# Gate and up projections of an FFN as seven-product 2x2 block multiplications, with hidden tiles and x1 in DRAM

## The chip, the cores and the metric

The kernel runs on one core of one Trainium2 chip. The metric is the device time of one execution in microseconds (us). Engines are named as the profile names them: PE is TensorE (matmuls; PEld its weight loads), DVE is VectorE, ACT is ScalarE, POOL is GpSimd, SP is SyncE, which only issues DMAs here. ACT issues DMAs too.

## The reference, cut to what matters

One layer of an encoder for 1024 prompt tokens and 64 sample tokens, which the kernel treats as one axis of 1088 tokens. Three token mixers (stick-breaking attention, RG-LRU, memory attention) are merged and projected; the change touches what follows:

```
x = x + merged @ lw["w_out"]                     # 1088 x 1024
xn2 = rms_norm(x, lw["norm_ffn_g"])
f = (silu(xn2 @ w_ffn_gate) * (xn2 @ w_ffn_up)) @ w_ffn_down   # hidden width 2816 = 22 x 128
x = x + f
```

## The kernel before

Activations lie feature-major: 8 tiles of 128 features x 1088 tokens. Every fp32 operand is split into a high and a low part (`split`, L68 and L69: ACT casts, DVE subtracts), and a product is three matmuls: high x high, high x low, low x high (`mm3`, L97 to L99). A projection tile (`proj`) is 128 output features: 3 column chunks of 364, 364 and 360 tokens, 8 contraction blocks and 3 matmuls, 72 in all.

The stages run one after the other: attention, RG-LRU, memory attention, branch merge, w_out, FFN. The program is written in that order, and a scheduler sets the order of instructions on each engine from data dependences, buffers and priorities; what each engine then does is fixed, in order. Names of tiles: `wo0` to `wo7` are the weights of the eight w_out tiles, `fg`, `fu` and `fd` those of gate, up and down; a last letter r is the raw load, h and l are the two parts. `xr` is a block of the input x, transposed by PE into `xtp` and copied by ACT to `mg`; `xrs` is that of the sample tokens.

In w_out (L926 to L958) each tile's evacuation adds the product to `mg` (x1), scales and splits it into `xg`, and POOL sums the squares in `ssq`. `token_scale` makes from these the 1/rms of each token, `R`: PE sums over features (`stp`), POOL takes the power (`rt`), PE spreads it (`rbp`). `raw` buffers, of which there are three, hold `ssq`, the `xr` blocks and raw weights. In the FFN gate and up tiles alternate; gate's evacuation is times R and Silu, up's is times R, times gate's tile on POOL, and split into `hh` and `hl`. After 6, 6, 6 and 4 hidden tiles the down projection of that group is added to `mg`; with the last group each tile is transposed (`ytp`) and stored.

## Time and profile before

| | us |
|---|---|
| timed runs | 2463.35, 2464.81, 2465.91 (median 2464.81) |
| profiled execution, span | 2465.6 |
| PE busy in the span | 2422.1 |
| DVE, ACT, POOL busy in the span | 1063.9, 850.3, 391.4 |

The span is that of the instructions of one execution, and it lies within the timed runs, so nothing of note lies around it. Busy shares are averages over stages with different limits; PE's matmul records overlap their successors, so that the rate is read from starts and not from durations.

### The profile page before, as it was taken

The page shows a single profiled execution, that of the slowest core. Times are in us where ns is not written, and L with a number is a line of the kernel's source. Part 1 is how long each engine was busy: PE and PEld are TensorE (multiplying, and loading weights), DVE is VectorE, ACT ScalarE, POOL GpSimd, SP SyncE. Part 2 cuts the span into 40 slices and gives each one's busy share as a digit, 9 for nine tenths or more (in the row PEclk, how much of TensorE's full clock was granted, in tenths as well). Part 3 has the DMA queues.
Part 4 walks back from the last instruction along what each step waited for, and adds up shares of the span by engine and source line. Part 5 has one row for each costly group of instructions (what it writes and reads, how often), then busy time and mean ns, then how long its engine had stood idle before and what let it go on. Part 6 is the DMA issues. An engine that isn't in the chain of part 4 may idle for free.

```text
span 2465.6 us, 36133 instructions
## 1 busy us (share of the span) xinstructions
PE 2422.1 (98%) x15030; PEld 2375.9 (96%) x15030; DVE 1063.9 (43%) x1715; ACT 850.3 (34%) x1484; POOL 391.4 (16%) x448
## 2 busy tenths in 40 slices
PE   7999999999999999999999999999999999999999
PEld 7899999989999999999989999999999999999999
DVE  4666666664555543333444323343323332332332
ACT  4555555554345333332354323222211221121112
POOL 3222222211112110100100222341100110010010
PEclk9999999999999999999999999999999999999999
DMA  4111111122322322222335432221111111111103
GB/s 144 55 56 56 56 56 56 56 69 81 106 85 87 105 88 92 85 78 93 109 117 175 148 100 83 80 79 43 42 39 58 43 35 52 44 46 39 53 26 90
DMA packets 281016, 185.16 MB, mean 75 GB/s; under 512 B 13059, under 2 KB 275414, under 8 KB 280854
## 3 DMA queue, kind: packets, MB, share of 16 engines
q10 hardware_dynamic: 209982, 108.36, 15.3%
q1 hardware_dynamic: 70872, 74.50, 9.3%
q8 instruction: 118, 1.93, 0.3%
q14 instruction: 44, 0.36, 0.0%
...
## 4 chain that ended last, share of the span: by engine, by line
PE 77%; DVE 1%; ACT 0%; issue 0%; POOL 0%; DMA 0%; ACTq 0%; DVEq 0%
PE mm L97 23%; PE mm L99 23%; PE mm L98 23%; PE mmk L97 1%; PE mmk L98 1%; PE mmk L99 1%; PE ytp L1033 0%; PE sc L97 0%; PE avm L97 0%; PE sc L98 0%; PE sc L99 0%; PE ptp L785 0%; PE gt L99 0%; PE gt L97 0%; PE avm L99 0%; PE avm L98 0%
## 5 line engine op out<-in xcount | busy, mean ns | idle before, releaser
L1006 POOL TENSOR_TENSOR ut<-ut,sil 128x364 f32<-128x364 f32 (+1 forms) x66 | 64.2, 973 | 670.1 <-DVE ut L1005 661.0
L1022 DVE TENSOR_TENSOR mg<-mg,mm 128x364 f32<-128x364 f32 (+1 forms) x96 | 51.1, 532 | 183.7 <-PE mm L99 183.7
L987 DVE TENSOR_TENSOR sil<-mm,R 128x364 f32<-128x364 f32 (+1 forms) x66 | 35.2, 535 | 163.3 <-PE mm L99 163.3
L68 ACT CAST hh<-ut 128x364 fp32r<-128x364 f32 (+1 forms) x66 | 32.8, 497 | 191.6 <-POOL ut L1006 191.6
L370 DVE TENSOR_TENSOR_SCAN e<-ones,e 128x128 f32<-128x128 f32 (+3 forms) x64 | 97.1, 1526 | 0.8
L852 POOL TENSOR_TENSOR mg<-mg,sig 128x364 f32<-128x364 f32 (+1 forms) x48 | 46.3, 968 | 286.1 <-DVE sig L851 286.1
L206 DVE TENSOR_SCALAR gst<-mm,prm 128x364 f32<-128x364 f32 (+1 forms) x71 | 42.0, 592 | 103.5 <-PE mm L99 103.5
L988 ACT ACTIVATE sil<-sil 128x364 f32<-128x364 f32 (+1 forms) x66 | 33.3, 506 | 128.2 <-DVE sil L987 128.1
L369 DVE SCALAR_TENSOR_TENSOR e<-z,e 128x384 f32<-128x384 f32 (+4 forms) x96 | 50.4, 553 | 61.3 <-ACT e L367 57.6
L1005 DVE TENSOR_TENSOR ut<-mm,R 128x364 f32<-128x364 f32 (+1 forms) x66 | 35.4, 536 | 95.8 <-PE mm L99 95.8
L846 ACT ACTIVATE sig<-sig 128x364 f32<-128x364 f32 (+1 forms) x72 | 35.8, 507 | 113.4 <-DMA sig<-g 102.5
L69 DVE TENSOR_TENSOR hl<-ut,hh 128x364 fp32r<-128x364 f32 (+1 forms) x66 | 35.1, 532 | 75.2 <-ACT hh L68 75.2
L374 ACT ACTIVATE e<-e 128x128 f32<-128x128 f32 (+3 forms) x64 | 43.9, 686 | 60.1 <-DVE e L373 52.3
L69 DVE TENSOR_TENSOR al<-at,ah 128x128 fp32r<-128x128 f32 (+2 forms) x96 | 51.1, 547 | 20.6 <-ACT ah L68 20.6
L97 PE MATMUL z<-kh,qh 128*128 128x384 f32 (+4 forms) x96 | 36.5, 380 | 14.7 <-DVE e L373 14.7
L365 ACT ACTIVATE e<-z 128x384 f32<-128x384 f32 (+4 forms) x96 | 45.7, 484 | 10.6 <-PE z L99 7.6
L373 DVE TENSOR_TENSOR e<-z,e 128x384 f32<-128x384 f32 (+4 forms) x96 | 48.9, 542 | 0.0
L98 PE MATMUL av<-al,vh 128*128 128x256 f32 x160 | 46.7, 292 | 0.2
L97 PE MATMUL av<-ah,vh 128*128 128x256 f32 x160 | 46.4, 290 | 0.4 <-ACT ah L68 0.4
L851 DVE TENSOR_TENSOR sig<-sig,mm 128x364 f32<-128x364 f32 (+1 forms) x48 | 25.2, 531 | 49.8 <-PE mm L99 49.7
L423 PE MATMUL at<-ident,e 128*128 128x128 f32 x288 | 45.1, 275 | 1.4 <-ACT ah L68 0.6
L68 ACT CAST ah<-at 128x128 fp32r<-128x128 f32 (+2 forms) x96 | 43.0, 471 | 10.0 <-PE at L423 10.0
...
## 6 DMA issues: line engine op xcount, KB each, us to landing
...
```

The lines of the kernel that those rows point to most:

```text
L68: (h_eng or S.copy)(h, src)
L69: (l_eng or V).tensor_sub(l, src, f32(h))
L97: TE.matmul(out, lh, rh, start=start, stop=False)
L98: TE.matmul(out, lh, rl, start=False, stop=False)
L99: TE.matmul(out, ll, rh, start=False, stop=stop)
L365: S.activation(ev, z, AF.Abs)
L369: V.scalar_tensor_tensor(ev, z, 0.0, ev, op0=ALU.max, op1=ALU.add)
L370: V.tensor_tensor_scan(e[:, ::-1], ones1[:n].to_broadcast([n, L]), e[:, ::-1], 0.0, op0=ALU.mult, op1=ALU.add)
L373: V.tensor_sub(ev, z, ev)
L852: G.tensor_add(dst, dst, st[:, :n])
L1006: G.tensor_mul(u, u, t)
L1022: V.tensor_add(mg[f][:, s:s + n], mg[f][:, s:s + n], p)
```

## The change

The gate and up weights of two neighbouring tiles (256 output features) and the 8 contraction blocks are taken as a 2x2 block matrix: A11, A12, A21, A22, where the first index is the output tile and the second parts even from odd contraction blocks. The activations are a 2x2 block matrix too: even and odd contraction blocks, and the two token halves of 544. Seven products of sums of these blocks (`PAIRS`) replace eight. The weight sums S1 to S4 and the activation sums T1 to T4 are formed on DVE in fp32 and then split as before. Each product has 2 column halves of 272 tokens, 4 contraction blocks and 3 matmuls; partial results are kept by ACT copies (`swt`) or accumulate in PSUM.

The 28 activation operands (7 kinds x 4) fill the tiles A and most of B, so the hidden tiles go to DRAM (`hid_scr`) and come back for the down projection, now in groups of 8, 8 and 6; x1 goes to `x1_scr` and comes back as `y`. The scaled x1 lies in `mg`, for the last two tiles in two `raw` buffers (`xg6`, `xg7`). The gate and up weights are loaded on SP's queue instead of ACT's, 256 features at a time. `form_early` runs with every second w_out tile, `form_late` behind the last. A parameter of the program that sets a scratch size for DMAs changes too.

```diff
+    PAIRS = (("A11", "B11"), ("S3", "T3"), ("S2", "T2"), ("A22", "T4"), ("S1", "T1"), ("A12", "B21"), ("S4", "B22"))
+    def sw_weights(src, name, slot, stage):
+        n = src.shape[0] // (2 * P)
+        v = src.rearrange("(i two p) f -> two p i f", two=2, p=P)
+        quads = {}
+        for r in range(2):
+            st = stage(f"{name}r{r}")[:, : 2 * n * P].rearrange("p (i f) -> p i f", i=n)
+            ST.dma_start(st, v[r])
+            quads[f"A1{r + 1}"], quads[f"A2{r + 1}"] = st[:, :, :P], st[:, :, P:]
+        for r in range(2):
+            st = stage(f"{name}s{r}")[:, : 2 * n * P].rearrange("p (x i f) -> p x i f", x=2, i=n)
+            for x, o in enumerate((("S3", "S2"), ("S1", "S4"))[r]):
+                quads[o] = st[:, x]
+        W = {}
+        def put(o):
+            w = W[o] = slot(f"{name}{o}")[:, : 2 * n * P].rearrange("p (x i f) -> p x i f", x=2, i=n)
+            split(w[:, 0], w[:, 1], quads[o])
+        put("A11")
+        V.tensor_sub(quads["S3"], quads["A11"], quads["A21"])
+        put("S3")
+        V.tensor_sub(quads["S2"], quads["A22"], quads["S3"])
+        put("S2")
+        V.tensor_add(quads["S1"], quads["A22"], quads["A21"])
+        put("A22")
+        put("S1")
+        V.tensor_sub(quads["S4"], quads["A12"], quads["S2"])
+        put("A12")
+        put("S4")
+        return W
+    def sw_product(W, X, n, banks, temp, out):
+        def run(op, bank, start):
+            a, b = PAIRS[op]
+            for c in range(2):
+                cs = slice(c * HC, (c + 1) * HC)
+                for i in range(n):
+                    w, x = W[a], X[b][i]
+                    for j, (wj, xj) in enumerate(((0, 0), (0, 1), (1, 0))):
+                        TE.matmul(bank[c][:, :HC], w[:, wj, i], x[:, xj, cs], start=start and i == 0 and j == 0,
+                                  stop=i == n - 1 and j == 2, skip_group_check=True)
+                yield c
+        def keep(bank, c, j):
+            with tc.high_priority():
+                S.copy(tmp[c][:, j], bank[c][:, :HC])
+        def done(f, half, bank, c, j):
+            with tc.high_priority():
+                out(f, half, c, bank[c][:, :HC], None if j is None else tmp[c][:, j])
+        bx, bw = banks(), banks()
+        tmp = [temp()[:, : 4 * HC].rearrange("p (j n) -> p j n", j=4) for _ in range(2)]
+        for c in run(0, bx, True):
+            keep(bx, c, 0)
+        for c in run(1, bw, True):
+            keep(bw, c, 1)
+        for c in run(2, bx, False):
+            keep(bx, c, 2)
+        for c in run(3, bw, False):
+            done(1, 0, bw, c, 2)
+        for c in run(4, bx, False):
+            done(1, 1, bx, c, 1)
+        by = banks()
+        for c in run(5, by, True):
+            done(0, 0, by, c, 0)
+        for c in run(6, bx, False):
+            done(0, 1, bx, c, None)
...
+        def operand(o, i, src):
+            t = XS[o][i] = at(xg_place[o, i], f"xg{o}{i}").rearrange("p (x n) -> p x n", x=2)
+            split(t[:, 0], t[:, 1], src)
+        def stage_x(name):
+            return wpl.tile([P, HT], F32, tag="stg", name=name, bufs=3)
+        def form_early(i, x0, x1):
+            operand("B11", i, x0[:, :HT])
+            t3, t2, t4 = (stage_x(f"t{j}{i}") for j in (3, 2, 4))
+            V.tensor_sub(t3, x1[:, HT:], x0[:, HT:])
+            operand("T3", i, t3)
+            V.tensor_add(t2, t3, x0[:, :HT])
+            operand("T2", i, t2)
+            V.tensor_sub(t4, x1[:, :HT], t2)
+            operand("T4", i, t4)
+        def form_late(i, x0, x1):
+            t1 = stage_x(f"t1{i}")
+            V.tensor_sub(t1, x0[:, HT:], x0[:, :HT])
+            operand("T1", i, t1)
+            operand("B21", i, x1[:, :HT])
+            operand("B22", i, x1[:, HT:])
...
+            ST.dma_start(x1_scr[f], mg[f])
+            x = mg[f]
+            if f >= KT - 2:
+                x = wpl.tile([P, T], F32, tag="raw", name=f"xg{f}", bufs=RAWB)
+            S.activation(x, mg[f], AF.Copy, scale=gk)
+            xg.append(x)
+            if f % 2 == 1:
+                form_early(f // 2, xg[f - 1], xg[f])
+        for i in range(KT // 2):
+            form_late(i, xg[2 * i], xg[2 * i + 1])
+        R = mgp.tile([P, T], F32, tag="mg0", name="R")
...
+        W_PLACES = [(wpl, "wh"), (wpl, "wl"), (wpl, "wh"), (wpl, "wl")] + PB[12:14]
+        STAGE_PLACES = [(wpl, "wx"), (wpl, "wx"), (wpl, "wx"), (mgp, "mg1"), (wpl, "wx"), (wpl, "wx"), (wpl, "wx"), PB[14]]
...
+        def temp():
+            return wpl.tile([P, T], F32, tag="raw", name="swt", bufs=RAWB)
+        def banks4():
+            pool, tag = cycle("b", [(psm, "mm"), (ps, "mm"), (ps, "mm"), (ps, "tr")])
+            return [pool.tile([P, 512], F32, tag=tag, name="sw", bufs=4 if pool is ps and tag == "mm" else 2)
+                    for _ in range(2)]
...
+        def up_pair(j, W, sil):
+            u = [at(cycle("u", U_PLACES), f"u{j}{f}", F32) for f in range(2)]
+            def out(f, half, c, p, other):
+                s = slice(half * HT + c * HC, half * HT + (c + 1) * HC)
+                t = u[f][:, s]
+                if other is None:
+                    V.tensor_mul(t, p, R[:, s])
+                else:
+                    V.tensor_add(t, p, other)
+                    G.tensor_mul(t, t, R[:, s])
+                V.tensor_mul(t, t, sil[f][:, s])
+            sw_product(W, XS, KT // 2, banks4, temp, out)
+            for f in range(2):
+                ST.dma_start(hid_scr[2 * j + f], u[f])
+        w = ffn_weights(w_ffn_gate, 0, "fg")
+        token_scale()
+        for j in range(NH // 2):
+            wu = ffn_weights(w_ffn_up, j, "fu")
+            sil = gate_pair(j, w)
+            if j + 1 < NH // 2:
+                w = ffn_weights(w_ffn_gate, j + 1, "fg")
+            up_pair(j, wu, sil)
+        groups = [list(range(0, 8)), list(range(8, 16)), list(range(16, 22))]
...
+        def load_h(j):
+            q = 2 * (j % 16)
+            Hh[j] = at((PA + PB)[q], f"hh{j}")
+            Hl[j] = at((PA + PB)[q + 1], f"hl{j}")
+            raw = wpl.tile([P, T], F32, tag="wx", name=f"hr{j}", bufs=3)
+            ST.dma_start(raw, hid_scr[j])
+            split(Hh[j], Hl[j], raw)
+        for j in groups[0]:
+            load_h(j)
+        mg = []
+        for f in range(KT):
+            mg.append(mgp.tile([P, T], F32, tag=f"mg{f}", name=f"y{f}"))
+            ST.dma_start(mg[f], x1_scr[f])
...
-    nc = bacc.Bacc("TRN2", target_bir_lowering=False, num_devices=1)
+    nc = bacc.Bacc("TRN2", target_bir_lowering=False, num_devices=1, dynamic_dma_scratch_size=2048)
```


Three places where the order of instructions differs. Names are as above; a number behind a name counts buffers.

ACT, around the turn from w_out's seventh tile (wo6) to its eighth (wo7). Before:

```order
L68 CAST wo6h_15735<-wo6r_15733 128x1024
L930 DMA xr7_15832<-in_x_prompt_dram 128x8x128
L948 ACTIVATE xgh5_15000<-mg5_9648,prm_150 128x364
L941 COPY mg6_9649<-xtp_15718 128x512
L948 ACTIVATE xgh5_15000<-mg5_9648,prm_150 128x360
L932 DMA xrs6_15716<-in_x_sample_dram 64x128
L941 COPY mg6_9649<-xtp_15724 128x512
L76 DMA wo7r_15851<-in_w_out_dram 128x8x128
L941 COPY mg6_9649<-xtp_15730 128x64
L948 ACTIVATE xgh6_15001<-mg6_9649,prm_150 128x364
L68 CAST wo7h_15853<-wo7r_15851 128x1024
```


After:

```order
L1064 COPY mg6_9649<-xtp_15774 128x64
L1083 ACTIVATE xg6_15871<-mg6_9649,prm_150 128x1088
L1053 DMA xr7_15873<-in_x_prompt_dram 128x8x128
L1055 DMA xrs7_15875<-in_x_sample_dram 64x128
L72 CAST xgB113_15988<-xg6_15871 128x544
L1064 COPY mg7_9650<-xtp_15877 128x512
L1064 COPY mg7_9650<-xtp_15883 128x512
L1064 COPY mg7_9650<-xtp_15889 128x64
L80 DMA wo7r_15892<-in_w_out_dram 128x8x128
L72 CAST wo7h_15894<-wo7r_15892 128x1024
L72 CAST fg0A11_16057<-fg0r0_16051 128x512
```


The load xr7 stood before, behind the cast of wo6, and wo7r amid the copies for wo6. Now the load xr7 stands behind the scaling that makes xg6 from the finished mg6, and wo7r behind the three copies of xr7's transposes, directly ahead of its cast.

PE, from the sums of squares to the spread of R. Before, with the first matmuls of up tile 0 (fu0) between:

```order
L967 MATMUL stp_16034<-ones1_82,ssq_15011 64x1
L97 MATMUL mm_16080<-xgh0_14995,fu0h_16076 128x364
L98 MATMUL mm_16080<-xgl0_15003,fu0h_16076 128x364
L99 MATMUL mm_16080<-xgh0_14995,fu0l_16077 128x364
L97 MATMUL mm_16080<-xgh1_14996,fu0h_16076 128x364
L98 MATMUL mm_16080<-xgl1_15004,fu0h_16076 128x364
L978 MATMUL rbp_16051<-ident_70,rt_16048 128x128 x4
L978 MATMUL rbp_16057<-ident_70,rt_16048 128x128 x4
```


After, a piece of the first gate pair, with the products of S2, A22 and S1 (the letters and digits behind fg0 name the weight block, xgT and the like the activation operand):

```order
L226 MATMUL sw_16148<-xgT22_15751,fg0S2_16065 128x272 x3
L226 MATMUL sw_16148<-xgT23_15999,fg0S2_16065 128x272 x3
L226 MATMUL sw_16150<-xgT40_15263,fg0A22_16069 128x272 x2
L226 MATMUL sw_16147<-xgT10_16008,fg0S1_16072 128x272 x2
L226 MATMUL sw_16148<-xgT10_16008,fg0S1_16072 128x272 x2
L226 MATMUL sw_16149<-xgT40_15263,fg0A22_16069 128x272
L226 MATMUL sw_16149<-xgT41_15509,fg0A22_16069 128x272 x3
L226 MATMUL sw_16149<-xgT42_15755,fg0A22_16069 128x272 x3
```


and further on:

```order
L226 MATMUL sw_16148<-xgT10_16008,fg0S1_16072 128x272
L226 MATMUL sw_16148<-xgT11_16019,fg0S1_16072 128x272 x3
L226 MATMUL sw_16148<-xgT12_16030,fg0S1_16072 128x272 x3
L1108 MATMUL rbp_16099<-ident_70,rt_16096 128x128 x4
L1108 MATMUL rbp_16105<-ident_70,rt_16096 128x128 x4
L226 MATMUL sw_16148<-xgT13_16041,fg0S1_16072 128x272 x3
L226 MATMUL sw_16291<-xgB210_16011,fg0A12_16076 128x272
```


The sums (`stp`) now stand around the first product (not shown); the spread (`rbp`) has moved from behind 5 matmuls of fu0 into the fifth product of the first gate pair. The first matmuls with S1 stand ahead of the rest of A22's.

DVE, from the token scale to the first evacuations. Before, `rt` follows at once on the last part of w_out:

```order
L947 TENSOR_TENSOR mg7_9650<-mg7_9650,mm_15919 128x360
L69 TENSOR_TENSOR fu0l_16077<-fu0r_16074,fu0h_16076 128x1024
L949 SCALAR_TENSOR_TENSOR xgl7_15010<-mg7_9650,prm_150,xgh7_15002 128x360
L970 COPY st_16044<-stp_16034 128x8
L971 COPY st_16044<-stp_16034 64x1
L176 TENSOR_SCALAR rt_16048<-st_16044 128x9
L69 TENSOR_TENSOR fg1l_16171<-fg1r_16168,fg1h_16170 128x1024
```


After, the rows that end at the first weight sums behind w_out:

```order
L73 TENSOR_TENSOR xgT11_16019<-t11_16017,xgT11_16019 128x544
L1042 TENSOR_TENSOR t13_16039<-xg6_15871 128x544
L73 TENSOR_TENSOR xgT12_16030<-t12_16028,xgT12_16030 128x544
L73 TENSOR_TENSOR xgB223_16047<-xg7_15986,xgB223_16047 128x544
L209 TENSOR_TENSOR fg0s1_16056<-fg0r1_16053,fg0r0_16051 128x512
L73 TENSOR_TENSOR xgT13_16041<-t13_16039,xgT13_16041 128x544
L73 TENSOR_TENSOR fg0A22_16069<-fg0r1_16053,fg0A22_16069 128x512
L73 TENSOR_TENSOR fg0S1_16072<-fg0s1_16056,fg0S1_16072 128x512
```


and those that end at `rt`:

```order
L1153 TENSOR_TENSOR sil01_16146<-sw_16149,swt_16151 128x272
L73 TENSOR_TENSOR fg0S4_16079<-fg0s1_16056,fg0S4_16079 128x512
L1153 TENSOR_TENSOR sil01_16146<-sw_16150,swt_16152 128x272
L1100 COPY st_16092<-stp_16082 128x8
L1101 COPY st_16092<-stp_16082 64x1
L73 TENSOR_TENSOR fu0A11_16120<-fu0r0_16114,fu0A11_16120 128x512
L1153 TENSOR_TENSOR sil01_16146<-sw_16147,swt_16151 128x272
L259 TENSOR_SCALAR rt_16096<-st_16092 128x9
```


Between the last evacuation of w_out (`mg7` plus `mm`) and the first sum `fg0s1` (L209) there are now 18 operations of 512 or 544 columns, and `rt` stands 13 rows behind that sum.

## Rows read from the trace of the kernel before

**Rows 1.** The page, busy us of each engine, share of the span, instructions

```profile
PE 2422.1 (98%) x15030; PEld 2375.9 (96%) x15030; DVE 1063.9 (43%) x1715; ACT 850.3 (34%) x1484; POOL 391.4 (16%) x448
```

**Rows 2.** The page, the chain of waits by line, shares of the span

```profile
PE mm L97 23%; PE mm L99 23%; PE mm L98 23%; PE mmk L97 1%; PE mmk L98 1%; PE mmk L99 1%; PE ytp L1033 0%; PE sc L97 0%; PE avm L97 0%; PE sc L98 0%; PE sc L99 0%; PE ptp L785 0%; PE gt L99 0%; PE gt L97 0%; PE avm L99 0%; PE avm L98 0%
```

**Rows 3.** Table by stage: us, busy (instructions) by engine, clock, DMA share, GB/s

```profile
1690.00:2395.00 705.00, 705.00 (x4248) 705.00 (x4247) 220.16 (x322) 122.58 (x188) 58.04 (x60) 1.00 0.15 44
```

**Rows 4.** Order of time, PE: start, us, line, tiles, shape

```profile
1998.27 0.32 PE L97 MATMUL mm<-xgh,fg11h 128*128 128x364 f32 x1
...
2010.23 0.33 PE L97 MATMUL mm<-xgh,fu11h 128*128 128x364 f32 x1
```

**Rows 5.** Order of time, PE, a run of 256 columns and what follows

```profile
586.66 0.28 PE L97 MATMUL mmk<-mTh,wm00h 128*128 128x256 f32 x1
...
589.54 0.32 PE L97 MATMUL mm<-Ah,wgl0h 128*128 128x364 f32 x1
```

**Rows 6.** Order of time, ACT, while the eighth tile of w_out starts

```profile
1629.70 0.60 ACT L948 ACTIVATE xgh<-mg,prm 128x360 fp32r<-128x360 f32 x1
1630.20 0.58 ACT L941 COPY mg<-xtp 128x512 f32<-128x512 f32 x1
...
1635.19 1.04 ACT L68 CAST wo7h<-wo7r 128x1024 fp32r<-128x1024 f32 x1
```

**Rows 7.** Order of time, ACT's queue, the load of fg3r

```profile
1690.26 0.38 ACTq L76 DMA_DIRECT2D fg3r<-in_w_ffn_gate_dram  x1
```

**Rows 8.** Table by stage around that load

```profile
1691.30:1693.80 2.50, 2.50 (x17) 2.50 (x17) 0.54 (x1) 0.51 (x1) 0.00 (x0) 1.00 0.73 210
1693.80:1697.00 3.20, 3.20 (x21) 3.20 (x21) 0.54 (x1) 0.51 (x1) 0.00 (x0) 1.00 0.00 0
```

**Rows 9.** Order of time, PE, eight transposes

```profile
1641.83 1.04 PE L937 MATMUL xtp<-ident,xr 128*128 128x128 f32 x8
```

**Rows 10.** Order of time, DVE, the low half of wo7

```profile
1636.27 1.57 DVE L69 TENSOR_TENSOR wo7l<-wo7r,wo7h 128x1024 fp32r<-128x1024 f32 x1 [0.34 <-ACT wo7h L68]
```

**Rows 11.** Table by stage around PE's longest idle time

```profile
1239.30:1245.00 5.70, 0.00 (x0) 0.00 (x0) 3.04 (x6) 2.14 (x2) 0.00 (x0) 0.94 0.95 291
1245.00:1251.10 6.10, 6.05 (x20) 5.89 (x21) 1.60 (x3) 4.57 (x8) 0.00 (x0) 0.50 0.41 138
1251.10:1257.10 6.00, 6.00 (x41) 5.98 (x40) 3.48 (x9) 2.16 (x6) 0.00 (x0) 1.00 0.70 208
```

**Rows 12.** The tiles fd30l and fg5l: their split, ns min/median/max

```profile
L69 DVE TENSOR_TENSOR fd30l<-fd30r,fd30h x1: 691/691/691, 2393.2 to 2393.2; 128x512 fp32r<-128x512 f32 x1
...
L69 DVE TENSOR_TENSOR fg5l<-fg5r,fg5h x1: 1226/1226/1226, 1772.3 to 1772.3; 128x1024 fp32r<-128x1024 f32 x1
```

**Rows 13.** Order of time, token scale: PE's sums, POOL's power

```profile
1667.05 2.05 PE L967 MATMUL stp<-ones,ssq 128*128 128x1 f32 x18
...
1669.65 2.71 POOL L177 TENSOR_TENSOR rt<-rt,mhalf 128x9 f32<-128x9 f32 x1 [11.01 <-DVE rt L176]
```

**Rows 14.** PE's waits from 1600 to 2395 us: total, times, longest

```profile
PE rbp L978 <- POOL rt L177: 2.3, 1, 2.3
```

**Rows 15.** Table by stage behind that wait

```profile
1671.00:1674.40 3.40, 1.99 (x9) 1.99 (x10) 0.69 (x1) 1.28 (x1) 1.36 (x1) 0.50 0.90 266
1674.40:1677.80 3.40, 3.40 (x11) 2.88 (x11) 1.96 (x5) 0.56 (x2) 0.00 (x0) 0.50 0.04 11
```

**Rows 16.** Groups by line, ACT, 1690 to 2395 us: busy, mean ns, idle before

```profile
L988 ACT ACTIVATE sil<-sil 128x364 f32<-128x364 f32 (+1 forms) x63 | 31.9, 506 | 123.4 <-DVE sil L987 123.3
L68 ACT CAST hh<-ut 128x364 fp32r<-128x364 f32 (+1 forms) x60 | 29.8, 497 | 175.1 <-POOL ut L1006 175.1
```

**Rows 17.** The same for DVE

```profile
L987 DVE TENSOR_TENSOR sil<-mm,R 128x364 f32<-128x364 f32 (+1 forms) x63 | 33.8, 536 | 163.3 <-PE mm L99 163.3
...
L69 DVE TENSOR_TENSOR fu1l<-fu1r,fu1h 128x1024 fp32r<-128x1024 f32 x1 | 1.8, 1810 | 0.4 <-ACT fu1h L68 0.4
```

**Rows 18.** The same for POOL

```profile
L1006 POOL TENSOR_TENSOR ut<-ut,sil 128x364 f32<-128x364 f32 (+1 forms) x60 | 58.0, 967 | 635.2 <-DVE ut L1005 626.1 <-ACT fd10h L68 3.0 <-ACT fd20h L68 3.0
```

More of the change, by code (lines that the diff above doesn't have):

```diff
@@ L922, with at @@
             now4(branch(2, f, w_br_mem, X2, done=XM))
-        XG = act_tiles("xg")
+        x1_scr = [drm.tile([P, T], F32, name=f"x1_{k}") for k in range(KT)]
+        hid_scr = [drm.tile([P, T], F32, name=f"hid{k}") for k in range(FFN // P)]
+        PA = [(act, f"A{x}{k}") for k in range(KT) for x in "hl"]
+        PB = [(bp, f"B{x}{k}") for k in range(KT) for x in "hl"]
+        def at(place, name, dt=F32R):
+            return place[0].tile([P, T], dt, tag=place[1], name=name)
+        xg_place = {}
+        for oi, (_, o) in enumerate(PAIRS):
+            for i in range(KT // 2):
+                xg_place[o, i] = (PA + PB)[oi * (KT // 2) + i]
+        XS = {o: [None] * (KT // 2) for _, o in PAIRS}
+        def operand(o, i, src):
[18 more added lines that the diff above has]
+            operand("B22", i, x1[:, HT:])
         ssq = wpl.tile([P, T], F32, tag="raw", name="ssq", bufs=RAWB)
+        xg = []
         for f in range(KT):
@@ L958 @@
             proj4(load_w(w_out[0, :, f * P:(f + 1) * P], f"wo{f}"), XM, ev)
-        R = bp.tile([P, T], F32, tag="Bh7", name="R")
+            ST.dma_start(x1_scr[f], mg[f])
[6 more added lines that the diff above has]
+                form_early(f // 2, xg[f - 1], xg[f])
+        for i in range(KT // 2):
+            form_late(i, xg[2 * i], xg[2 * i + 1])
+        R = mgp.tile([P, T], F32, tag="mg0", name="R")
         def token_scale():
@@ L980, in token_scale, with cycle @@
                 V.tensor_copy(R[:, g * 512:g * 512 + n], p[:, :n])
-        def ffn_gate(j, before=None):
-            sil = bp.tile([P, T], F32, tag=("Bh6", "Bl6")[j % 2], name=f"sil{j}")
-            def ev(ci, s, n, p):
-                t = sil[:, s:s + n]
-                V.tensor_mul(t, p, R[:, s:s + n])
+        turn = {"w": 0, "s": 0, "b": 0, "u": 0}
+        def cycle(key, places):
+            turn[key] += 1
+            return places[(turn[key] - 1) % len(places)]
+        W_PLACES = [(wpl, "wh"), (wpl, "wl"), (wpl, "wh"), (wpl, "wl")] + PB[12:14]
@@ L1011, with out @@
-        groups = [list(range(0, 6)), list(range(6, 12)), list(range(12, 18)), list(range(18, 22))]
-        sil = ffn_gate(0, before=token_scale)
+        def up_pair(j, W, sil):
+            u = [at(cycle("u", U_PLACES), f"u{j}{f}", F32) for f in range(2)]
+            def out(f, half, c, p, other):
+                s = slice(half * HT + c * HC, half * HT + (c + 1) * HC)
+                t = u[f][:, s]
+                if other is None:
+                    V.tensor_mul(t, p, R[:, s])
+                else:
+                    V.tensor_add(t, p, other)
+                    G.tensor_mul(t, t, R[:, s])
+                V.tensor_mul(t, t, sil[f][:, s])
+            sw_product(W, XS, KT // 2, banks4, temp, out)
+            for f in range(2):
+                ST.dma_start(hid_scr[2 * j + f], u[f])
```

48 lines of the change are left out of this document (24 added, 24 removed).

## The prediction

> **What bounds the kernel now.** I read the busy shares first, then the chain of waits, then the table by stage, then single rows. TensorE (PE) is busy for 2422.1 of 2465.6 us [rows 1], and the chain that ended last runs through the projection matmuls of L97 to L99, 23% of the span each [rows 2]. Between 1690 and 2395 us, which is nearly all of the FFN, PE is busy for 705.00 of 705.00 us; DVE has 220.16, ACT 122.58, POOL 58.04 and the DMA engines a share of 0.15 [rows 3]. So FFN time is the number of matmuls times their spacing, and another engine counts only where it makes PE wait. The spacing is read from starts, since matmul records overlap: the 72 matmuls of tile fg11 take from 1998.27 to 2010.23 us, 0.1661 us each at 363 columns on average [rows 4].
>
> The rows come from one execution with a span of 2465.6 us; the three timed runs lie at 2463.35 to 2465.91 with a median of 2464.81. I make the sum on the span and take 0.8 us off.
>
> **Term 1, the matmuls: -57.1 us.** Before, gate and up are 44 tiles of 72 matmuls: 3168 x 0.1661 = 526.2 us. After, there are 22 pairs of tiles, each with seven products of 2 column halves x 4 contraction blocks x 3 = 24 matmuls of 272 columns: 22 x 168 = 3696. No row has 272 columns. A run of 24 matmuls with 256 columns takes from 586.66 to 589.54, 0.1200 each [rows 5]. A line through 256 and 363 columns gives 0.1200 + 16 x 0.000432 = 0.1269, so 469.1 us. Scaling the 256 row by columns gives 0.1275 (471.2 us), scaling the 363 row 0.1246 (460.4 us): the gain lies between 55 and 66 us. I take 57.1, since 256 is the nearest width. The down projection keeps 1584 matmuls of the same shape.
>
> **Term 2, the turn from the seventh to the eighth tile of w_out: +15 us.** The scaled x1 of the last two tiles (xg6, xg7) now takes a "raw" buffer, of which there are three; ssq holds one. The order of ACT shows what follows: before, wo7r is loaded during wo6; now ACT issues the load xr7 only behind the scaling of xg6, which needs wo6's last evacuation, and wo7r goes into xr7's buffer, so it is issued behind the copies of xr7's transposes. PE's next instructions are those transposes and then wo7, so PE waits for the whole row of steps. From the end of wo6's last matmul:
> evacuation with hand-over 0.75; scaling of 1088 columns 1.2 (0.60 for 360 and 1.04 for 1024 columns [rows 6]); xr7 from issue to the end of its packets 3.55 (fg3r, of the same size and packets: issued at 1690.26, DMA busy from 1691.3 to 1693.8 [rows 7, 8]); nine transposes, 1.04 for eight at full clock [rows 9], 1.5 here; the copies behind them 0.9 (0.58 each [rows 6]); wo7r 3.55; its cast 1.04 and low half 1.4 (1.57 beside POOL [rows 10]). Sum 13.9, less 1.04 for transposes that were there before and 0.66 for four matmuls that need the high half alone: 12.2 us. ACT's casts behind wo7r wait too, but they belong to the FFN and come in time.
> Then the clock. Where PE had stood idle from 1239.3 to 1245.0, the granted clock was 0.50 (1.2 GHz) for the next 6.1 us with 20 matmuls, against 41 in the 6.0 us after it at 1.00 (2.4 GHz) [rows 11]; that restart cost 6.1 - 20 x 6.0 / 41 = 3.2 us. I add 2.8. Bounds: 0 if wo7r were on time, 20 with both idle stretches followed by a slow one.
>
> **Term 3, the first gate pair: +3.7 us.** The seven right-hand operands are split by ACT and DVE, and part of that lies behind wo7. In DVE's order 17 operations of 544 columns, 2 of 512 and the last evacuation (0.73 us with its hand-over) stand up to the sum S1 of the first weights. A 512-column subtraction takes 0.691 and a 1024-column one 1.226 [rows 12], so 544 take 0.725: 17 x 0.725 + 2 x 0.691 + 0.73 = 14.5 us after wo7, and with ACT's cast 15.1. PE gets there after 9 token sums (2.05 us [rows 13]) and 80 matmuls (10.2 us), at 12.2: it waits 2.9. Thirteen more rows of DVE, 7.0 us, lead up to rt, and POOL needs 2.71 for it [rows 13], so 24.2; PE, with 41 matmuls behind S1's cast, is there at 20.3 and waits 3.9. Half a clock behind these two waits costs some 1.6. Against these 8.4 us goes what leaves: 2.3 us in which PE waits for POOL's rt [rows 14], and a clock of 0.50 until 1677.8, with 11 matmuls in 3.40 us [rows 15] where 20 fit; that and the eight transposes are 2.4 us. Bounds: -4.7 if all is hidden, +12 if the slow clock follows each wait in full.
>
> **Term 4, the steady pairs: 0.** PE needs 168 x 0.1269 = 21.3 us for a pair. For a gate pair ACT has 7 casts, 6 copies and 8 Silu, by 0.50 and 0.51 us for 364 columns [rows 16] about 10 us; DVE has 11 operations of 512 columns (7.6 us) and 8 evacuations of 272 columns (0.44 each, from 0.536 for 364 [rows 17]), 11.1 us. For an up pair DVE has 8 products more: 14.4 us, and it waits six times for POOL's multiplication (0.73 us, from 0.967 [rows 18], with hand-overs 0.95). In its order three of these waits are filled with a weight operation; the rest, 3 x 0.95 us, makes 17.3. That is under 21.3. Each weight slot comes free six products ahead, each bank has a product's time (3.0 us) to be evacuated, and the weights now go through SP's queue behind the stores of the hidden tiles, 3.6 us each against 15 us of lead. Traffic to DRAM grows by 2 x (22 + 8) x 0.56 = 33 MB over 720 us, 46 GB/s beside 44 [rows 3].
> One edit could spoil that: fu1l took 1.810 us where fg5l took 1.226 for the same shape [rows 12, 17]. The Trainium skill (SBUF — State Buffer, Who interferes with whom) says that a VectorE instruction with two SBUF inputs and a GpSimd instruction that reads SBUF exclude each other for a whole instruction. By that rule six POOL operations could hold up an up pair by 6 x 0.73 us, to 21.7 us, and the time would be 5 us longer; the trace agrees with the 0.58 us of fu1l.
>
> **Term 5, small ones: +2 us.** Loading fg0's first weights now stands early in the program, with two DVE operations between the steps of x's norm: 0.7. At the first down tile the low half fd00l stands behind seven splits of hidden tiles: 0.7. The x1 stores delay the scaling of earlier tiles and so a small transpose in wo2 and wo4; by the same 3.55 us it just arrives: 0.5. Bounds 0 and 6.
>
> **Sum.** -57.1 + 15 + 3.7 + 2 = -36.4, so 2429.2 us on the span and 2428.4 as a median.
>
> **Rivals.**
> A. The turn of term 2 is short, because a buffer or the ACT order lets wo7r come earlier: then 2413 to 2416 us. For it: nothing in the order; against it: the load stands behind copies that need PE. 10%.
> B. DVE is late in the up pairs: every POOL operation collides, each by the 0.58 us of fu1l, and no wait is filled: 14.4 + 5.7 + 3.5 = 23.6 us, 2.3 over PE, times 11 is 25 us: 2453 us. For it: fu1l; against it: POOL is busy in a fifth of the pair only. 14%.
> C. It ends slower: a matmul's spacing has a large part that does not shrink with its columns. Eight transposes of 128 columns start 0.11 us apart (1.04 less 0.27 for the last record, by seven [rows 9]), twice what their columns would take by the 0.1661 row. A line from there to 363 columns gives 0.144 at 272: 3696 x 0.144 = 532 us, 6 more than before, with terms 2, 3 and 5 2492 us. It decides from 0.137 on, where 3696 matmuls have used up the 36 us. Against it: 0.1200 at 256 columns, in a run of 24 with the same three-product pattern. 4%.
> The Trainium skill (TensorE: Matmul & The Clock Gate, Back-to-back issue gap) speaks for C: it gives a sustained 81 ns per matmul at 128 columns and 131 at 512, both set by weight load and matmul together. By a line between them 272 columns would cost 0.89 of 363, 3696 matmuls 4% more than 3168, and the sum would end near 2508 us, an estimate. The trace disagrees: 256 columns cost 0.72 of 363 here [rows 4, 5].
> The forecast has 72%.
>
> **From this the numbers.** Likeliest 2428. The range 2408 to 2454 takes in A and B and the bounds of terms 1 and 3. By 0.2%, about 5 us, a measurement of this kernel tells a change: faster 0.93, within it 0.02, slower 0.05.
>
> **What would show it.** Right: 3696 matmuls 0.125 to 0.130 us apart, PE with no idle time inside the pairs after the first, a wait of 10 to 15 us ahead of wo7 put down to ACT's cast or the DMA of wo7r, with a clock of 0.50 behind it, and two waits of 2 to 5 us in the first gate pair, for ACT's S1 and POOL's rt. Wrong: a spacing over 0.135; idle PE in each up pair, ended by DVE or ACT; or w_out as tight as before.

## The result and the profile after

The changed kernel takes 2431.34 us (median of four runs, 2427.29 to 2433.35) where the kernel before takes 2465.22: ratio 0.9857, 95% interval 0.9843 to 0.9871. Forecast were 2428 us, and 2408 to 2454 as the range. The profiled execution has a span of 2427.8 us and, as a timed run, 2429.91; how spans and medians go together stands at the end of this section.

The page's busy time and chain, as in [rows 1, 2], of the changed kernel:

```profile
PE 2361.8 (97%) x15558; PEld 2313.5 (95%) x15558; DVE 1191.9 (49%) x1989; ACT 945.0 (39%) x1708; POOL 450.9 (19%) x514
...
PE sw L226 18%; PE mm L101 16%; PE mm L102 16%; PE mm L103 16%; PE mmk L101 1%; PE mmk L103 1%; PE mmk L102 1%; PE ytp L1223 0%; PE avm L101 0%; PE ptp L868 0%; PE sc L103 0%; PE sc L102 0%; PE sc L101 0%; PE gt L101 0%; PE gt L103 0%
```

The three lines of `proj` (one for each of a product's three matmuls) have fallen from 23% of the span each to 16%, and the products' one line (L226) has 18%. The table by stage over the pairs behind the first (fu0 to fg10), which answers to [rows 3]:

```profile
1700.00:2121.90 421.90, 421.90 (x3373) 421.90 (x3373) 254.32 (x466) 158.76 (x346) 111.67 (x122) 1.00 0.26 83
```

PE is as full as before. DVE's share has doubled (254 of 422 us, before 220 of 705 in a stretch that holds down tiles too), POOL's has tripled, and the traffic is 83 GB/s where 44 + 46 = 90 was expected. The spacing, from starts as in [rows 4], in the first product of an up pair:

```profile
1785.55 3.16 PE L226 MATMUL sw<-xgB,fu2A 128*128 128x272 f32 x24
1788.55 0.66 PE L226 MATMUL sw<-xgT,fu2S 128*128 128x272 f32 x4
```

24 matmuls of 272 columns in 3.00 us are 0.1250 each, and a pair is 21.02 us long. What PE waits for from 1600 us on, which is within w_out (total, times, longest, us):

```profile
PE xtp L1060 <- DMA xr<-in_x_prompt_dram: 6.0, 1, 6.0
PE mm L101 <- ACT wo7h L72: 4.9, 1, 4.9
PE mm L103 <- DVE fd00l L73: 4.4, 1, 4.4
PE sw L226 <- ACT swt L232: 2.9, 1, 2.9
PE rbp L1108 <- POOL rt L260: 2.0, 1, 2.0
PE xtp L1062 <- DMA xrs<-in_x_sample_dram: 1.3, 2, 0.8
PE stp L1097 <- POOL ssq L1076: 1.1, 1, 1.1
PE sw L226 <- DVE u L1169: 0.4, 1, 0.4
```

The two first lines are the turn to the eighth tile of w_out; the third is the first down tile; the next two are the first gate pair. Then come the blocks of sample tokens in w_out, the token sums and the last up pair. From first starts of tiles in both traces, the span's 37.8 us split up so (the line of wo6 and wo7 ends at the first token sum, 1.0 us ahead of fg0's first product in the changed kernel):

| stretch | before | after | difference |
|---|---|---|---|
| up to w_out (wo0) | 1549.9 | 1545.2 | -4.7 |
| w_out, tiles wo0 to wo5 | 79.5 | 81.5 | +2.0 |
| w_out, wo6 and wo7 | 25.7 | 40.5 | +14.8 |
| token sums and the first gate pair, over the steady time | 8.3 | 13.2 | +4.9 |
| gate and up at the steady time (44 x 11.975, 22 x 21.023) | 526.9 | 462.5 | -64.4 |
| last up pair, over the steady time | 0 | 0.7 | +0.7 |
| first down tile, over the steady time | 0 | 6.8 | +6.8 |
| the other down tiles, and the end | | | +2.1 |

The first line is not traced to the change. PE's order there differs in a dozen rows near the start only; but the execution before has two stretches at half clock in which PE was busy throughout, and the one after has none there (stretch, its length, busy time and instructions of PE, PEld, DVE, ACT, POOL, clock, DMA share, GB/s; the kernel before, then after):

```profile
1039.50:1042.90 3.40, 3.40 (x15) 3.40 (x14) 0.17 (x1) 0.00 (x0) 1.55 (x1) 0.50 0.52 154
1196.50:1199.90 3.40, 3.40 (x13) 3.40 (x12) 0.36 (x3) 0.00 (x0) 1.81 (x1) 0.50 0.65 180
```

```profile
1039.50:1042.90 3.40, 3.40 (x25) 3.40 (x24) 1.20 (x5) 0.69 (x2) 1.78 (x1) 1.00 0.53 154
1196.50:1199.90 3.40, 3.40 (x25) 3.40 (x24) 1.70 (x6) 1.03 (x3) 0.76 (x1) 1.00 0.57 212
```

Each cost about 1.7 us, together 3.4 of the 4.7. Both profiled executions of the changed kernel (the second is e7 below) have no such stretch, and wo0 starts at 1545.3 and 1544.9 us; each of the ten variants has one to three, and wo0 starts between 1547.4 and 1553.4, also in the five whose order of PE up to there is that of the changed kernel. The timed runs of the changed kernel differ likewise: mean granted clocks of 0.993, 0.991, 0.990 and 0.989 go with spans of 2425.2, 2427.8, 2430.6 and 2431.2 us. So I take the line for a difference between executions; with one or two profiles of a kernel that is not proved.

Ahead of the prediction the span before is said to lie within the timed runs, with nothing of note around it. That is not so: where a run's time and span are both known, the time is 1.7 to 2.3 us longer (2429.91 against 2427.8). The span of 2465.6 thus belongs to a run of some 2467.5 us (an estimate), about 2.3 slower than the median before, and the execution after is 1.4 faster than its median. That is why the two profiled executions lie 37.8 us apart and the medians 33.9.

### The profile page after: what moved, and what is told of

The parts are those of the page before. It is cut to its first block, busy times and chain, and to the rows that moved or that the text cites. A ratio compares the mean times of both kernels' runs of the same rounds, so it can differ in the third digit from the quotient of the medians.

```text
span 2427.8 us, 37941 instructions
## 1 busy us (share of the span) xinstructions
PE 2361.8 (97%) x15558; PEld 2313.5 (95%) x15558; DVE 1191.9 (49%) x1989; ACT 945.0 (39%) x1708; POOL 450.9 (19%) x514
## 4 chain that ended last, share of the span: by engine, by line
PE 72%; DMA 2%; DVE 2%; ACT 1%; POOL 1%; issue 1%; ACTq 0%; DVEq 0%; POOLq 0%; SPq 0%
PE sw L226 18%; PE mm L101 16%; PE mm L102 16%; PE mm L103 16%; PE mmk L101 1%; PE mmk L103 1%; PE mmk L102 1%; PE ytp L1223 0%; PE avm L101 0%; PE ptp L868 0%; PE sc L103 0%; PE sc L102 0%; PE sc L101 0%; PE gt L101 0%; PE gt L103 0%
## 5 line engine op out<-in xcount | busy, mean ns | idle before, releaser
L1212 DVE TENSOR_TENSOR y<-y,mm 128x364 f32<-128x364 f32 (+1 forms) x72 | 38.2, 531 | 177.5 <-PE mm L103 174.9
L1170 POOL TENSOR_TENSOR u<-u,R 128x272 f32<-128x272 f32 x66 | 69.6, 1057 | 185.2 <-DVE u L1169 185.2
L232 ACT COPY swt<-sw 128x272 f32<-128x272 f32 x132 | 50.9, 387 | 108.4 <-PE sw L226 94.8
L1154 POOL TENSOR_TENSOR sil<-sil,R 128x272 f32<-128x272 f32 x66 | 53.2, 808 | 146.7 <-DVE sil L1153 143.6
L1155 ACT ACTIVATE sil<-sil 128x272 f32<-128x272 f32 x88 | 37.5, 431 | 69.5 <-POOL sil L1154 65.8
L1171 DVE TENSOR_TENSOR u<-u,sil 128x272 f32<-128x272 f32 x88 | 39.9, 456 | 45.4 <-POOL u L1170 44.8
L740 POOL TENSOR_TENSOR ig<-ig,xc 128x1092 f32<-128x1092 f32 x8 | 20.4, 2554 | 131.4 <-ACT ig L732 131.4
```

The lines of the kernel that those rows point to most:

```text
L232: S.copy(tmp[c][:, j], bank[c][:, :HC])
L1154: G.tensor_mul(t, t, R[:, s])
L1170: G.tensor_mul(t, t, R[:, s])
```

## The experiments

All times are medians of runs beside runs of the kernel before on the same chip (which took 2465.3 to 2465.6). Unless a name says otherwise, a variant is the changed kernel with the edit shown. An interval is some 7 us wide, so smaller differences between variants are read from stretches of their profiles.

| run | us | ratio to before, 95% interval |
|---|---|---|
| e7 changed kernel again | 2431.51 | 0.9862 (0.9845 to 0.9878) |
| e1 own buffer for wo6r, wo7r | 2419.66 | 0.9813 (0.9799 to 0.9828) |
| e2 down weight first | 2426.94 | 0.9843 (0.9828 to 0.9858) |
| e3 T1 on POOL | 2435.04 | 0.9876 (0.9861 to 0.9891) |
| e4 half width | 3534.87 | 1.4339 (1.4315 to 1.4363) |
| e5 fill | 2429.83 | 0.9849 (0.9834 to 0.9864) |
| e6 POOL twice | 2466.07 | 1.0002 (0.9992 to 1.0011) |
| e8 repaired | 2440.40 | 0.9894 (0.9880 to 0.9909) |
| e9 both | 2415.44 | 0.9792 (0.9778 to 0.9805) |
| e10 R early | 2416.92 | 0.9797 (0.9784 to 0.9811) |
| e11 weights first | 2424.27 | 0.9831 (0.9817 to 0.9844) |

**The changed kernel again (e7).**

> The changed kernel itself, unaltered, beside the others on the same chip: 2431 us, with the waits of its first profile (6.0, 4.9, 4.4, 2.9 and 2.0 us) in the same places; stretches of half clock ahead of w_out differ between executions by some 3 us.

It has the same waits, 6.0, 4.8, 4.4, 2.9 and 2.0 us, and steady pairs of 21.02 us. They belong to the kernel and not to one execution.

**The turn in w_out (e1).** How it went in the changed kernel, in order of time on ACT's queue, PE and ACT:

```profile
1639.99 1.20 ACT L1083 ACTIVATE xg<-mg,prm 128x1088 f32<-128x1088 f32 x1 [3.44 <-DVE mg L1070]
1639.99 0.42 ACTq L1053 DMA_DIRECT2D xr<-in_x_prompt_dram  x1
1645.31 1.94 PE L1060 MATMUL xtp<-ident,xr 128*128 128x128 f32 x8 [5.99 <-DMA xr<-in_x_prompt_dram]
1647.59 0.37 ACTq L80 DMA_DIRECT2D wo7r<-in_w_out_dram  x1
1651.36 1.04 ACT L72 CAST wo7h<-wo7r 128x1024 fp32r<-128x1024 f32 x1 [3.37 <-DMA wo7r<-in_w_out_dram]
1652.46 0.67 PE L101 MATMUL mm<-xmh,wo7h 128*128 128x364 f32 x1 [4.91 <-ACT wo7h L72]
```

The load of xr7 is issued as soon as the last evacuation lets ACT issue it, beside the scaling and not behind it, and takes 5.3 us to arrive; then come the transposes at half clock, the copies, the load of wo7 and its cast. The edit:

```diff
+            if f >= KT - 2:
+                wr = wpl.tile([P, T], F32, tag="wx", name=f"wo{f}r", bufs=3)[:, :D].rearrange(...)
+                LD.dma_start(wr, src.rearrange("(k p) n -> p k n", p=P))
-            proj4(load_w(src, f"wo{f}"), XM, ev)
+            proj4(load_w(src, f"wo{f}", raw=wr), XM, ev)
```

> The raw loads of wo6 and wo7 go to another set of buffers (the one that the FFN's weights use later), so that wo7r no longer takes the buffer of xr7; in ACT's order its cast now stands ahead of the copies for tile 6, and in PE's order the transposes of xr7 have moved from ahead of wo7 to 34 matmuls behind its start. My theory (the two waits of 6.0 and 4.9 us ahead of wo7 come from that buffer, and the half clock behind them from the waits): both go, the clock is 1.00 from wo6 to the end of wo7, wo6 and wo7 together take 26 to 27 us instead of 40.5, at most 1 us of wait is left for xr7; time 2415 to 2419 us where the changed kernel has 2431. Rival: x's and the weights' loads are late because x1's stores and the loads share the DMA engines; then a wait of 4 to 6 us for xr7 or wo7r stays and the time is 2423 to 2428.

Up to fg0's first product wo6 and wo7 take 27.3 us (41.5 in the changed kernel), the clock stays at 1.00 (second fence), and one wait is left:

```profile
PE xtp L1060 <- DMA xr<-in_x_prompt_dram: 0.5, 1, 0.5
```

```profile
1641.50:1658.10 16.60, 16.13 (x103) 15.56 (x101) 7.18 (x10) 7.55 (x14) 7.82 (x9) 1.00 0.25 69
```

The theory holds, with a time a little over the 2415 to 2419 us expected: 11.8 us of the changed kernel are one buffer with two users. The rival's wait of 4 to 6 us did not stay.

**The first down tile (e2).** In the changed kernel DVE worked through the last up pair like this, in its order:

```profile
2143.88 0.99 DVE L1171 TENSOR_TENSOR u<-u,sil 128x272 f32<-128x272 f32 x1 [0.32 <-POOL u L1170]
2144.79 1.28 DVE L73 TENSOR_TENSOR hl<-hr,hh 128x1088 fp32r<-128x1088 f32 x1
...
2146.69 1.77 DVE L73 TENSOR_TENSOR fd00l<-fd00r,fd00h 128x1024 fp32r<-128x1024 f32 x1
```

fd00l stood behind a multiplication that waited for POOL and behind the split of a hidden tile, and then took 1.77 us beside POOL. The edit asks for its weights ahead of the hidden tiles:

```diff
+        fd00 = load_w(w_ffn_down[0, :KT * P, :P], "fd00")
         for j in groups[0]:
             load_h(j)
```

> The first down tile's weights are asked for ahead of the eight hidden tiles; in DVE's order its low half fd00l moves from behind the split of the eighth hidden tile and four evacuations of the last up pair to ahead of the seventh's split. My theory (fd00l is late because of its place in DVE's order): the wait of 4.4 us and the 2.4 us of half clock behind it fall to 0 to 1.5 us together, first down tile 12 to 13.5 us instead of 18.8; time 2425 us, 5 to 6.5 less. Rival: DVE waits there for POOL's multiplications of the last up pair, whatever the order; the wait then stays over 3 us, or goes to the split of the eighth hidden tile, and the time is within 2 us of the changed kernel's.

The first down tile takes 14.3 us instead of 18.8 (12 to 13.5 expected), the last up pair 21.02 instead of 21.68. The wait has shrunk and moved to the split of a hidden tile, as the rival had it in part:

```profile
PE mm L102 <- DVE hl L73: 2.0, 1, 2.0
```

**The first gate pair (e3).** Where the first wait there ended, DVE, ACT and PE of the changed kernel:

```profile
1680.84 0.71 DVE L1042 TENSOR_TENSOR t<-xg 128x544 f32<-128x544 f32 x1
1681.59 0.68 ACT L232 COPY swt<-sw 128x272 f32<-128x272 f32 x2 [0.63 <-DVE t L1042]
1682.03 1.40 PE L226 MATMUL sw<-xgT,fg0S 128*128 128x272 f32 x6 [2.92 <-ACT swt L232]
```

PE waits for a copy of a PSUM bank (the memory that matmuls write to), and ACT for DVE's fourth T1 block. The likely reason, read from the order and not tested alone: that copy goes into the raw buffer that xg6 held until this subtraction had read it. The edit takes the four subtractions off DVE:

```diff
-            V.tensor_sub(t1, x0[:, HT:], x0[:, :HT])
+            G.tensor_sub(t1, x0[:, HT:], x0[:, :HT])
```

> The four subtractions that make the T1 blocks behind w_out go from DVE to POOL. My theory (the waits of 2.9 and 2.0 us in the first gate pair come from DVE's backlog of 17 operations behind w_out; ACT's copies of the banks stand behind the casts of T1): 4 x 0.72 = 2.9 us of DVE go, the first wait falls to under 1 us, the second to under 0.5, the first gate pair takes 27 to 30 us instead of 33.2; time 2425 to 2428 us. Rival: POOL is slower at it (1.5 to 2 us each, behind the sums of squares) and the T1 blocks come no earlier; the waits stay at 4 to 6 us in total and the time within 2 us of the changed kernel's, or over it.

Nothing is won; the waits are 2.4 (now for S1), 2.0 and 1.5 us, the pair takes 34.8. What POOL does, DVE pays for:

```profile
1683.44 1.71 POOL L1042 TENSOR_TENSOR t<-mg 128x544 f32<-128x544 f32 x1 [0.73 <-DVE xgT L73]
1685.11 1.81 POOL L1042 TENSOR_TENSOR t<-xg 128x544 f32<-128x544 f32 x1
```

```profile
1681.44 4.29 DVE L73 TENSOR_TENSOR xgT<-t,xgT 128x544 fp32r<-128x544 f32 x3
1685.65 1.81 DVE L209 TENSOR_TENSOR fg0s<-fg0r,fg0r 128x512 f32<-128x512 f32 x1
```

In the changed kernel each of these splits takes 0.72 us and fg0s 0.68. Beside POOL the first and third of the three shown last 1.86 and 1.88, the T1 split ahead of them 1.77 and fg0s 1.81. Each of these four ends 0.54 to 0.59 us behind the end of the POOL operation beside it, as if DVE worked only when POOL was done.

**Width (e4).**

```diff
-                        TE.matmul(bank[c][:, :HC], w[:, wj, i], x[:, xj, cs], ...)
+                        for q in range(2):
+                            qs = slice(q * HC // 2, (q + 1) * HC // 2)
+                            TE.matmul(bank[c][:, qs], w[:, wj, i], x[:, xj, cs][:, qs], ...)
```

> Each matmul of the seven products is issued as two of 136 columns, so that the columns stay and the count doubles, 7392 for 3696. By the line through 272 columns (0.1251 us measured in the changed kernel) and 363 (0.1661) a matmul has a fixed part of 0.0025 us: 0.0638 at 136, 472 us instead of 462, time 2441 us. The rival of a large fixed part (line through the transposes, 0.11 us at 128 columns, and 363 columns): 0.112 at 136, 828 us, time 2797 us. Between them a floor at some width would show as a spacing of 0.07 to 0.10, 2486 to 2710 us.

(Its sums within a bank are not the reference's; count and shape of the instructions are as said.) Both theories were wrong, the rival less. At full clock nine such matmuls take 1.20 us:

```profile
1669.70 1.20 PE L228 MATMUL sw<-xgB,fg0A 128*128 128x136 f32 x9
```

That is about 0.11 us each, no faster than with 128 columns [rows 9]. By this the FFN would take some 350 us more. But it took 1100 more: behind a wait of PE for 2.1 us in the first gate pair (first line) the clock fell at 1673.6 us, and it stayed at 0.50 until the down projection, with PE never idle in the 21 pairs behind the first (second line is a piece):

```profile
1669.70:1673.60 3.90, 1.76 (x16) 1.62 (x16) 3.90 (x6) 3.20 (x5) 2.46 (x2) 1.00 0.35 143
1760.00:1850.00 90.00, 90.00 (x423) 90.00 (x424) 16.95 (x29) 8.37 (x18) 4.57 (x6) 0.50 0.10 31
```

423 matmuls in 90 us are 0.213 each. So a matmul has a floor of 0.11 us at full clock; 256 and 272 columns lie above it, and from there on the columns count. With 0.00046 us a column (0.1250 by 272) floor and columns meet near 240, an estimate. The token sums, with a single column, come no faster either (18 in 2.05 us [rows 13]). Each of these matmuls has its own weight load of 128 columns, and no run separates the two.

**The clock (e5).** 59 matmuls that nobody reads fill the two waits of the turn:

```diff
+            if f == KT - 1:
+                fill(mg[f - 1], 32)   # ahead of xr7's transposes
...
+                fill(mg[f], 27)       # ahead of wo7
```

> The changed kernel with 59 more matmuls of 364 columns whose results nobody reads: 32 between wo6 and the transposes of xr7 and 27 between these and wo7, each group behind one transpose that needs the finished mg6 or mg7, so that TensorE works in the two waits ahead of wo7 (6.0 and 4.9 us). My theory (the clock of 0.50 from 1641.5 to 1658.6 us comes from TensorE's idle time): the clock stays 1.00 there, the eight transposes take 1.04 us instead of 1.94 and the first 23 matmuls of wo7 start 0.166 us apart instead of 0.30; wo6 and wo7 together take 36 to 38 us instead of 41.5, and the time is 2426 to 2428 us. Rival: the clock falls there for another reason, whatever TensorE does; then wo6 and wo7 take 41 to 43 us and the time is 2431 to 2433.

```profile
1641.50:1667.80 26.30, 24.53 (x152) 23.91 (x152) 7.43 (x11) 8.59 (x15) 5.29 (x6) 1.00 0.23 64
1667.80:1702.80 35.00, 28.73 (x187) 27.72 (x187) 27.49 (x46) 16.55 (x31) 10.32 (x9) 0.85 0.19 62
```

The clock stays at 1.00 up to the end of wo7, so PE's idle time is what had lowered it there. Up to fg0's first product wo6 and wo7 take 39.1 us instead of 41.5, less of a gain than expected (36 to 38), and the first gate pair now has a third stretch at half clock and takes 35.0 instead of 33.2: the time is that of the changed kernel within the runs' spread.

**The margin of the up pairs (e6).**

```diff
+                    G.tensor_mul(wpl.tile([P, HT], F32, tag="stg", name="dup", bufs=3)[:, :HC], t, R[:, s])
                     G.tensor_mul(t, t, R[:, s])
```

> The changed kernel with each of POOL's six multiplications of an up pair done a second time into a buffer that nobody reads, ahead of the one that counts. In a steady up pair DVE is busy for 11.6 us and waits 4.4 for POOL; PE takes 21.0. My theory (the margin of DVE in an up pair is about 5 us, and each added multiplication of 1.05 us delays DVE by about its own length): DVE's path becomes 16.0 + 6.3 = 22.3 us, PE begins to wait in the up pairs, by 0 to 2 us each, and the time is 2431 to 2455 us. Rival (POOL's work is hidden in the order and has far more margin): no wait of PE in the pairs, 2431 us. The other rival (POOL and DVE keep each other from working, and every collision adds up): over 3 us of wait in each up pair, 2465 us or more.

All of the gain is gone, 35 us, more than my theory had. The time is that of the rival in which collisions add up, but it comes another way: not in each up pair, but in five of the ten steady gate pairs (fg1, fg3, fg5, fg7, fg9). They take 26.4 to 27.6 us, a wait of 3.8 us each with a stretch at half clock behind it, some 29 of the 35 us; the last up pair takes 24.3, and the others stay at 21.0. PE and DVE at one of the five:

```profile
1819.33 2.94 PE L226 MATMUL sw<-xgT,fg3S 128*128 128x272 f32 x13 [3.82 <-DVE u L1167]
```

```profile
1818.75 0.43 DVE L1167 TENSOR_TENSOR u<-sw,R 128x272 f32<-128x272 f32 x1
1819.22 0.44 DVE L1172 TENSOR_TENSOR u<-u,sil 128x272 f32<-128x272 f32 x1
```

PE's second product of the gate pair waits for the bank of one of the up pair's last evacuations. In the changed kernel the same two stand so, DVE and PE:

```profile
1808.03 0.43 DVE L1167 TENSOR_TENSOR u<-sw,R 128x272 f32<-128x272 f32 x1
1809.58 0.67 PE L226 MATMUL sw<-xgT,fg3S 128*128 128x272 f32 x4
```

That evacuation ends at 1808.46 and PE is there at 1809.58: the margin is 1.1 us in such a pair. The evacuations of an up pair all come with its last four products, each step DVE, POOL, DVE, so they lag behind PE's banks however little DVE has to do in the pair as a whole. POOL's step is longer than forecast too, 1057 ns as a mean in the changed kernel:

```profile
L1170 POOL TENSOR_TENSOR u<-u,R 128x272 f32<-128x272 f32 x66 | 69.6, 1057 | 185.2 <-DVE u L1169 185.2
```

**A version with both repairs (e9), and three that add more (e8, e10, e11).** e9 is the edits of e1 and e2.

> The edits of e1 and e2 alone (own buffers for the raw loads of wo6 and wo7; the first down tile's weights asked for first), with the products in their first order. If both gains are independent: the turn 26 to 28 us instead of 41.5, the first down tile 14.3 instead of 18.8, up pairs of 21.0 us again, 2431 - 12 - 5 = 2413 to 2416 us. If the 22.5 us of every up pair in e8 came from something else than the exchanged products, they stay here and the time is 2430 us.

It has the lowest median of all, within noise of e10's: the gains add up (16 us against the changed kernel again), wo6 and wo7 take 27.4 us, the first down tile 13.8, and the up pairs 21.02. The waits of 2.9 and 2.0 us in the first gate pair stay.

e8 was run before it, with three more edits at once. Its core:

```diff
+        by = banks()
+        for c in run(5, by, True):
+            done(0, 0, by, c, 0)
         for c in run(4, bx, False):
             done(1, 1, bx, c, 1)
-        by = banks()
-        for c in run(5, by, True):
-            done(0, 0, by, c, 0)
```

> The edits of e1 and e2 together, and three for the first gate pair: the first pair's kept partial results go to mg6 and mg7 instead of two raw buffers of which xg6 holds one until T1 is formed; the token scale is put ahead of the first gate weights and gets priority, so that rt stands 26 rows of DVE earlier; and the product A12 x B21 comes ahead of S1 x T1. Theory: the turn gives 14 us, the down tile 5, and in the first gate pair the waits of 2.9 and 2.0 us shrink to one of about 2 for rt, 3 to 5 us with their half clock; 2431 - 14 - 5 - 4 = 2408 us, range 2405 to 2414. Rival (the first pair is bound by DVE's work behind w_out, so that another wait of 3 to 5 us for T1 or S1 takes the place): 2412 to 2416 us.

It is slower than the changed kernel. Each up pair takes 22.5 us, since the last product now comes directly behind the one whose result DVE must first take from the same bank (A12 x B21 stood between), and waits for DVE:

```profile
1804.49 1.76 PE L226 MATMUL sw<-xgB,fu2S 128*128 128x272 f32 x12 [0.67 <-DVE u L1177]
1806.55 1.64 PE L226 MATMUL sw<-xgB,fu2S 128*128 128x272 f32 x11 [0.30 <-DVE u L1177]
```

e9, without the exchange, has pairs of 21.02 us, so the exchange costs 11 x 1.5 = 16.5 us: the small margin again. In the first gate pair waits of 4.5 us (for a low half of fg0's weights) and 3.7 (rt) took the place; it takes 39.6 us, and 31.6 in e9.

e10 is e9 with R taken into gate's tile, so that the up evacuations need no POOL:

```diff
                 S.activation(t, t, AF.Silu)
+                G.tensor_mul(t, t, R[:, s])
...
-                    G.tensor_mul(t, t, R[:, s])
-                V.tensor_mul(t, t, sil[f][:, s])
+                V.tensor_mul(t, p, sil[f][:, s])
```

> e9, and R is taken into gate's tile (POOL multiplies silu by R after Silu), so that an up evacuation is one addition and one multiplication on DVE and no longer waits for POOL; 2 multiplications of DVE per pair go as well. Theory (DVE, waiting for POOL in its order, is late only in the last up pair, where the splits of the hidden tiles come on top; elsewhere PE is the bound): the steady pairs stay 21.0 us, the wait of 2.0 us at the first down tile goes to under 0.5, with its half clock 2 to 3.7 us: 2410 to 2413 us. Rival (POOL was never late): the wait at the first down tile stays, the time is that of e9 within 1 us; or POOL's doubled work in the gate pairs now makes PE wait there, and the time is over 2416.

The time is that of e9 within noise. The wait at the first down tile is gone (11.98 us for the tile), but the last up pair takes 27.0 us. ACT and PE there:

```profile
2124.27 1.10 ACT L72 CAST hh<-hr 128x1088 fp32r<-128x1088 f32 x1 [6.06 <-DMA hr<-hid]
2125.27 0.38 ACT L232 COPY swt<-sw 128x272 f32<-128x272 f32 x1
```

```profile
2125.70 1.50 PE L226 MATMUL sw<-xgT,fu10S 128*128 128x272 f32 x5 [3.24 <-ACT swt L232]
```

In ACT's new order a hidden tile's cast, which waits 6.1 us for its load from DRAM, stands ahead of the copy that PE needs. The stall has changed engines, and neither the theory nor the rival had that.

e11 is e10 with fg0's weights formed ahead of T1 and B2 blocks, priority for the token scale, and mg6 and mg7 for the first kept results.

> e10, and three edits at the first gate pair: fg0's weights are formed ahead of the T1, B21 and B22 blocks in DVE's order, the token scale gets priority, and the pair's kept partial results go to mg6 and mg7. Theory (the waits of 2.9 and 2.0 us there are a matter of DVE's order behind w_out, where what PE needs first, A22 and S1, stands last): one wait of about 2 us for rt is left early in the pair, the first gate pair takes 28 to 30 us instead of 33.2, 3 to 5 us less than e10. Rival (DVE has too much to do behind w_out in any order): other waits of 4 us or more for T3, T4 or T1 take the place, the pair takes 33 us or more.

PE waits 7.4 us for rt, and here is why:

```profile
1666.80 7.80 POOL L260 TENSOR_TENSOR rt<-rt,mhalf 128x9 f32<-128x9 f32 x1 [2.11 <-DVE rt L259]
```

```profile
1674.65 1.76 PE L1110 MATMUL rbp<-ident,rt 128*128 128x128 f32 x7 [7.42 <-POOL rt L260]
```

POOL's power over nine columns, 2.71 us in [rows 13] and 2.17 in the changed kernel, takes 7.80 here. DVE subtracts without a break from 1666.6 to 1672.9 us, and the power ends 1.7 us behind that. The first gate pair's matmuls stretch over 36.7 us, with fu0's first among them. The rival was right on the pair's length (33 us or more), but the wait is for rt and not for a T block. In each order of this work that was tried, PE's waits here come to 5 us or more.

## Why the prediction was right, and where it was not

The way, the range and nearly the size were right, but the closeness of the sum (2428 forecast, 2431.34 measured) is luck: an error of 7 us in term 1 and one of 7 in term 5 cancel. The measured sizes below are those of the table, from one execution of each kernel.

- Term 1: 0.1269 us was taken, 0.1250 measured, within its bounds; with the old tiles at 11.975 us on average, the gain is 64 us and not 57. The step that failed is the choice of the nearest width: the 363-column row scaled by columns (0.1246) was nearer than the line from 256 columns (0.1269).
- Term 2: +15 forecast, +14.8 measured, and e1 shows the cause. Inside it errors cancel: the load of xr7 doesn't wait for the scaling (1.2 us), but takes 5.3 us and not 3.55. Idle time was 10.9 us (12.2), in two waits and not one, the clock about 4 (2.8).
- Term 3: +3.7 forecast, +4.9 measured. The wait of 2.9 us came out to the tenth by luck, for it was not for S1: PE stood one step earlier, at a copy whose raw buffer, by the order, xg6 still held. e3 shows S1 close behind it (2.4 us). rt cost 2.0 instead of 3.9, and two stretches of 3.4 us in the pair ran at half clock.
- Term 4: 0 forecast and measured in the steady pairs, but argued wrongly. I compared sums over a pair, 17.3 with 21.3 us; the evacuations crowd into the last four products, and the margin is 1.1 us (e6). POOL's multiplication took 1.06 us, more than the 0.73 to 0.95 put in. The 21.7 us a pair that collisions with POOL might have made did not come (21.02), but by that margin rival B was nearer than its 14% say.
- Term 5: +2 forecast, +8.8 measured. wo0 to wo5 gave +2.0 instead of +0.5, with four short waits for xrs. The early load cannot be told from the differences between executions. The first down tile gave +6.8 instead of +0.7, and here a step failed in its size. I had seen that fd00l stands behind the hidden tiles' splits and put 0.7 us; POOL's multiplications ahead of it in DVE's order, and the half clock behind the wait, were left out. e2 gives 4.5 of it back. The +2.1 of the other down tiles and the end was in no term, and its cause is open.
- Rival C: at 272 columns it is wrong, as the 256-column row said. Its fixed part is real: e4 finds the floor at 136 columns, 0.11 us. The Trainium skill (TensorE: Matmul & The Clock Gate, Back-to-back issue gap) has 81 ns at 128 columns and 131 at 512 for a sustained stream, but 0.11 us at 128 and 136 columns, 0.125 at 272 and 0.166 at 363 were measured with this kernel's operands, and the measurement decides.
- Rival A did not come by itself; e1 makes it (2413 to 2416 forecast, 2419.66 measured).
